# First layer's entry: x rows loaded first, the norm's squares between the columns, two convolutions in two token ranges

## The chip, the cores and the metric

The program runs on one core of a Trainium2 chip. A core has a matrix engine (TensorE, PE in the profile), and three engines that work on up to 128 partitions at once: VectorE (DVE), ScalarE (ACT) and GpSimd (POOL). SyncE (SP) issues most of the transfers between HBM and the on-chip memory SBUF; TensorE writes to a second memory, PSUM, which VectorE and ScalarE read. Each engine works through its own instructions in order and waits on semaphores for the others. The metric is the device time of one execution in microseconds (us), as the median of several runs.

## The reference

One step of a trunk with two layers: a Mamba-2 layer (SSD), then a layer of latent attention (MLA), each on a prompt of 1024 tokens and on a sample group of 8 x 8 tokens, 1088 tokens in all, of width 1024. The part that the change touches is the beginning of the first layer:

```python
def rms_norm(x, w):
    xf = x.astype(F32)
    y = xf * lax.rsqrt(jnp.mean(xf * xf, axis=-1, keepdims=True) + NORM_EPS)
    return (y * w.astype(F32)).astype(x.dtype)

def causal_conv(xbc, buf, w, b):
    t = xbc.shape[1]
    full = jnp.concatenate([buf.astype(xbc.dtype), xbc], axis=1)
    out = full[:, 0:t] * w[0]
    for k in range(1, SSD_CONV_W):
        out = out + full[:, k:k + t] * w[k]
    return out + b, full[:, full.shape[1] - (SSD_CONV_W - 1):]
...
def ssd_mixer(h, conv_buf, ssm_state, w_in, conv_w, conv_b, dt_bias, a_log, d_skip, norm_w, w_out):
    b, t, _ = h.shape
    proj = jnp.einsum('btd,de->bte', h, w_in)
    z = proj[..., :SSD_D_INNER]
    xbc = proj[..., SSD_D_INNER:SSD_D_INNER + SSD_CONV_DIM]
    dt_raw = proj[..., SSD_D_INNER + SSD_CONV_DIM:]
    xbc, new_buf = causal_conv(xbc, conv_buf, conv_w, conv_b)
    xbc = jax.nn.silu(xbc.astype(F32))
```

The rows x are normed by the root of their mean square, multiplied by the input weights, and 4096 of the resulting columns go through a causal convolution over four tokens and a SiLU. Everything is float32. The output of the whole is the normed result, the new SSM and convolution states and the new cache rows.

## The kernel before

A float32 product is made of three products of operands split in a high and a low part: high x high, low x high and high x low. So every operand is split: ScalarE writes the high part (for x: `xh`, for weights: `wih`), and VectorE or GpSimd the low part (`xl`, `wil`). The split of weights is at lines 129 and 130; the raw weights (`wraw`) come by a transfer at line 276.

The tokens are cut in three ranges, of 384, 384 and 320 tokens (range 0, 1 and 2), and in nine tiles of 128 rows (the last has 64), three tiles to a range. The norm of the first layer goes range by range (`norm_steps`). `norm_rows` loads a range's tiles `xt` (line 694 for the prompt, 696 for the sample group), lets ScalarE square each and sum it (line 223, result `ssq`), VectorE add the small constant (line 203), GpSimd raise it to the power -1/2 (line 208), and VectorE scale the rows (line 228). `norm_cols` then takes the eight groups of 128 columns, called columns 0 to 7 here: TensorE transposes the three tiles into PSUM (line 238, `xtp`, two buffers), ScalarE multiplies by the norm's weight and writes the high part (line 239, `xh`), VectorE the low part (line 240, `xl`). As columns of a range become ready, TensorE multiplies them with the first two blocks of weights (line 88, `pj`): six products to a column, three for each block. A block is 128 of the output columns. The blocks 0 and 1 of the first group run through all three ranges side by side with the norm; block 2 and the rest follow.

The rows of a range are normed while the range before is projected: in the program, `norm_rows` of range i + 1 is called behind `norm_cols` of range i. What a piece of product leaves in PSUM, ScalarE copies to a buffer `raw` (line 458 for ranges 0 and 1, 460 and 461 for range 2), of which there are two. When a block's three pieces are there, ScalarE begins the convolution (line 471: the last of four taps, with the bias), and VectorE adds the other three taps, one step each over 1112 columns (line 474). Only then is the buffer `raw` free for the next block but one: block 2 takes that of block 0. Between these stand, on VectorE, the low part of a weight block, and on GpSimd low parts of the weights of block 2 (line 130) and of the gates (line 335).

Other loads at the entry, in the order of the program: the identity `ident` (line 138), `alog` (line 160, with an exponential on ScalarE at line 161, which brings the loading of an activation table), the vectors of the convolution and the norms (lines 183 to 188), masks (167 to 173), `dtb` and `dsk` (175, 176), and the convolution's state `cst` (311), which TensorE transposes (line 316, `cvp`).

The order of an engine's instructions is set by a planner, which works from estimated costs of its own and from the program's order, unless a stretch of the program states for an engine that the written order stands (`manual_schedule`). Before the change that is used for two late places only. The same code of the norm serves the second layer (there with `tail`, line 864 being a gate beside it), and the planner orders that as well.

## Time and profile before

| | us |
|---|---|
| median of 3 runs | 2012.39 |
| lowest and highest run | 2009.29, 2013.6 |
| profiled execution | 2011.21 |
| its span in the profile | 2009.4 |
| TensorE busy | 1916.5 (95%) |
| VectorE busy | 1198.7 (60%) |
| ScalarE busy | 1109.7 (55%) |
| GpSimd busy | 826.6 (41%) |

The profile is one execution; its span is 1.8 us shorter than its device time. A row of a timeline gives start, length, engine, line, operation, output and inputs, and in brackets how long the engine was idle before it and what ended that. In rows of transfers, SPq is the queue of SyncE. "x3" puts three of a kind in a row together. A TensorE row's length reaches beyond the start of the next, since products overlap.

### The profile page before, as it was taken

The numbers are of one execution on the slowest core, as the hardware profiler recorded it, in microseconds if no ns is written. First come the engines' busy times: TensorE is split into PE (matmuls) and PEld (weight loads), VectorE is DVE, ScalarE is ACT, GpSimd is POOL, SyncE is SP. The second block draws the span as 40 slices with busy tenths as digits, with TensorE's granted clock in tenths as the row PEclk, the third lists the DMA queues.
The fourth block names the chain that finished last, engine by engine and source line by source line (L and its number), as shares of the span: only waits on it lengthen the run. The fifth ranks groups of instructions, "written<-read, shape, count | busy, mean of one in ns | idle before, by whom it ended". The sixth has DMA issues, their size and how long they took to land. (4 is left out here: it accounts for less than half of the span.)

```text
span 2009.4 us, 33417 instructions
## 1 busy us (share of the span) xinstructions
PE 1916.5 (95%) x12001; PEld 1739.9 (87%) x12001; DVE 1198.7 (60%) x2431; ACT 1109.7 (55%) x2535; POOL 826.6 (41%) x1007
## 2 busy tenths in 40 slices
PE   6999999999999999898998999999999999889998
PEld 5899999999999999786777999898888888778887
DVE  4537565656575656755333204465787877676675
ACT  5456767666666666733114314335777777655552
POOL 1327555555655555542002213103343435755551
PEclk9999999999999999899999999999999999899999
DMA  4213333333323332646544333132121113544541
GB/s 150 58 52 93 90 86 92 83 95 84 95 82 94 82 94 66 199 154 198 158 142 133 125 145 90 62 108 73 50 66 40 50 42 91 176 148 142 146 145 37
DMA packets 182460, 206.58 MB, mean 103 GB/s; under 512 B 18988, under 2 KB 147896, under 8 KB 181912
## 3 DMA queue, kind: packets, MB, share of 16 engines
q1 hardware_dynamic: 177240, 184.67, 30.9%
q0 software_dynamic: 4976, 19.66, 3.1%
q8 instruction: 95, 1.56, 0.3%
q14 instruction: 69, 0.57, 0.1%
q10 hardware_dynamic: 80, 0.13, 0.0%
HBM read 151.10 MB, written 53.28 MB: 102 GB/s over the span
## 5 line engine op out<-in xcount | busy, mean ns | idle before, releaser
L88 PE MATMUL pj<-xh,wih 128*128 128x384 f32 (+1 forms) x768 | 256.4, 338 | 9.5 <-ACT xh L239 4.9
L88 PE MATMUL pj<-xl,wih 128*128 128x384 f32 (+1 forms) x768 | 255.3, 333 | 0.0
L88 PE MATMUL pj<-xh,wil 128*128 128x384 f32 (+1 forms) x768 | 254.8, 332 | 0.0
L474 DVE SCALAR_TENSOR_TENSOR acc<-raw,vec,acc 128x1112 f32<-128x1112 f32 x96 | 141.2, 1475 | 25.7 <-ACT acc L471 24.9
L88 PEld LDWEIGHTS pj<-xh,wih 128*128 128x128 f32 x768 | 145.7, 191 | 11.7 <-ACT xh L239 5.5
L1283 POOL TENSOR_TENSOR tl<-P,th 128x384 fp32r<-128x384 f32 (+1 forms) x96 | 91.7, 956 | 155.4 <-ACT P L1281 113.6
L88 PEld LDWEIGHTS pj<-xl,wih 128*128 128x128 f32 x768 | 146.4, 191 | 0.9
L88 PEld LDWEIGHTS pj<-xh,wil 128*128 128x128 f32 x768 | 146.0, 190 | 0.4
L100 PE MATMUL pz<-wih,xh 128*128 128x256 f32 x504 | 142.5, 286 | 0.0
L100 PE MATMUL pz<-wil,xh 128*128 128x256 f32 (+1 forms) x504 | 140.1, 284 | 0.0
L1280 ACT ACTIVATE th<-st 128x512 fp32r<-128x512 f32 x192 | 94.5, 492 | 71.2 <-PE st L1276 52.0
L577 ACT ACTIVATE M<-M,tok 128x128 f32<-128x128 f32 (+1 forms) x288 | 90.6, 386 | 70.3 <-DVE M L574 69.8
L100 PE MATMUL pz<-wih,xl 128*128 128x256 f32 x448 | 128.3, 286 | 0.0
L1572 POOL TENSOR_TENSOR kvl<-pgr,kvh 128x1024 fp32r<-128x1024 f32 x32 | 77.6, 2426 | 70.5 <-ACT kvh L1571 70.5
L100 PEld LDWEIGHTS pz<-wih,xh 128*128 128x128 f32 x504 | 95.8, 190 | 0.3
L574 DVE TENSOR_TENSOR M<-M,negu 128x512 f32<-128x512 f32 x64 | 51.2, 800 | 70.7 <-DMA M<-acs_d 70.2
L1281 ACT ACTIVATE P<-st 128x512 f32<-128x512 f32 x192 | 93.4, 486 | 0.0
L100 PEld LDWEIGHTS pz<-wil,xh 128*128 128x128 f32 (+1 forms) x504 | 92.7, 184 | 0.8
L130 DVE TENSOR_TENSOR wil<-wraw,wih 128x512 fp32r<-128x512 f32 x88 | 71.6, 823 | 31.0 <-ACT wih L129 29.7
L1283 DVE TENSOR_TENSOR tl<-P,th 128x512 fp32r<-128x512 f32 x96 | 72.9, 759 | 21.5 <-ACT P L1281 20.8
L100 PEld LDWEIGHTS pz<-wih,xl 128*128 128x128 f32 x448 | 85.2, 190 | 0.1
L560 POOL TENSOR_TENSOR xdd<-xsT,tok 128x256 f32<-128x256 f32 x64 | 51.0, 797 | 73.3 <-ACT xsT L546 73.0
(820 smaller groups left out, 6326.8 us busy)
## 6 DMA issues: line engine op xcount, KB each, us to landing
wraw<-in_ssd_w_in SPq DMA_DIRECT2D x92, 256.0 KB
M<-acs_d SPq DMA_DIRECT2D x64, 256.0 KB
s<-in_state_ssm SPq DMA_DIRECT2D x32, 256.0 KB
y_d<-y SPq DMA_DIRECT2D x64, 128.0 KB
out_s_ssm<-s SPq DMA_DIRECT2D x32, 256.0 KB
wraw<-in_ssd_w_out SPq DMA_DIRECT2D x16, 512.0 KB
q_d<-qt SPq DMA_DIRECT2D x32, 192.0 KB
qp<-q_d SPq DMA_DIRECT2D x8, 768.0 KB
```

The lines of the kernel that those rows point to most:

```text
L88: nc.tensor.matmul(out, a, b, start=(i == 0), stop=(i == n - 1))
L100: nc.tensor.matmul(o, a, b, start=(j == 0), stop=(j == len(ops) - 1))
L130: (eng or nc.vector).tensor_tensor(lo, src, hi.bitcast(F32), op=ALU.subtract)
L474: nc.vector.scalar_tensor_tensor(acc, raw[:, j : j + n], k.convw[j][:, blk : blk + 1], acc, op0=ALU.mult, op1=ALU.add)
L560: nc.gpsimd.tensor_tensor(v3(xdd), v3(xsT), hb(2), op=ALU.mult)
L574: nc.vector.tensor_tensor(M[:m, :, :m], M[:m, :, :m], (k.negs if smp else k.negu)[:m, :m].unsqueeze(1).to_broadcast([m, 4, m]), op=ALU.add)
L577: nc.scalar.activation(M[:m, h, :m], M[:m, h, :m], AF.Exp, bias=tk[:, 0, 4 * g + h : 4 * g + h + 1])
L1280: nc.scalar.activation(th[:, :n], ps[:, :n], AF.Exp, scale=SCALE)
L1281: nc.scalar.activation(P[:, :n], ps[:, :n], AF.Exp, scale=SCALE)
L1283: eng.tensor_tensor(tl[:, :n], P[:, :n], th[:, :n].bitcast(F32), op=ALU.subtract)
L1572: nc.gpsimd.tensor_tensor(rl, raw, rh.bitcast(F32), op=ALU.subtract)
```

## The change

Three things are changed in the first layer's entry.

The transfers of the first three x tiles are issued ahead of those of `ident` and `alog`; `ident` now goes with the vectors, and `alog` and its exponential with the masks.

The square of a tile of the next range is no longer called behind all columns of the present range but between them: `norm_rows` becomes a generator (`rows_steps`), of which one step (a load and a square) follows each column from column 2 on (`LATE = 2`). In the first layer the whole norm stands under `manual_schedule` for ScalarE, so that ScalarE takes its instructions there in the order in which the program states them. In the second layer (`tail`) the steps are still taken behind the columns.

The convolutions of blocks 0 and 1 of the first group are done in two ranges of tokens: 768 columns as soon as ranges 0 and 1 are in `raw`, the other 344 at the end.

```diff
+LATE = 2
...
-    nc.sync.dma_start(k.ident, I["c_ident"])
...
-    nc.sync.dma_start(k.alog, k.I["ssd_a_log"][0].partition_broadcast(128))
-    nc.scalar.activation(k.alog, k.alog, AF.Exp)
...
     nc.gpsimd.memset(k.yssq, 1.0)
+    nc.sync.dma_start(k.alog, I["ssd_a_log"][0].partition_broadcast(128))
+    nc.scalar.activation(k.alog, k.alog, AF.Exp)
...
     nc, I, cp = k.nc, k.I, k.cp
+    nc.sync.dma_start(k.ident, I["c_ident"])
...
-def norm_rows(k, gi, load, pool, xbufs, pre=None):
+def norm_rows(*a):
+    xs = []
+    drain(rows_steps(xs, *a))
+    return xs
+
+
+def rows_steps(xs, k, gi, load, pool, xbufs, pre=None):
...
         xs.append((xt, m, TILES[i][0] - t0))
+        yield
...
     for gi in range(3):
-        norm_cols(k, gi, rows, wcol, hi, lo, psum)
-        if gi < 2:
-            rows = norm_rows(k, gi + 1, load, pool, xbufs, pre[gi + 1])
+        cols, nxt = norm_cols(k, gi, rows, wcol, hi, lo, psum), []
+        more = rows_steps(nxt, k, gi + 1, load, pool, xbufs, pre[gi + 1]) if gi < 2 else iter(())
+        for d, _ in enumerate(cols):
+            if not tail and d >= LATE:
+                next(more, None)
+        drain(more)
+        rows = nxt
...
+        def conv(a, b):
+            nc.scalar.activation(acc[:, a:b], raw[:, 3 + a : 3 + b], AF.Identity, bias=k.convb[:, blk : blk + 1],
+                                 scale=k.convw[3][:, blk : blk + 1])
+            for j in range(3):
+                nc.vector.scalar_tensor_tensor(acc[:, a:b], raw[:, j + a : j + b], k.convw[j][:, blk : blk + 1],
+                                               acc[:, a:b], op0=ALU.mult, op1=ALU.add)
+
         for ci in range(3):
             if ci == 2:
+                if g == 0 and bi < 2:
+                    conv(0, 768)
...
-        n = RAW - 3
-        nc.scalar.activation(acc, raw[:, 3:], AF.Identity, bias=k.convb[:, blk : blk + 1],
-                             scale=k.convw[3][:, blk : blk + 1])
-        for j in range(3):
-            nc.vector.scalar_tensor_tensor(acc, raw[:, j : j + n], k.convw[j][:, blk : blk + 1], acc,
-                                           op0=ALU.mult, op1=ALU.add)
+        conv(768 if g == 0 and bi < 2 else 0, RAW - 3)
...
-            norm_steps(k, x_loader(k), None, k.xh, k.xl, p0, psum, [st0], XB, before, after)
+            with tc.manual_schedule(engines={nc.scalar.engine}):
+                norm_steps(k, x_loader(k), None, k.xh, k.xl, p0, psum, [st0], XB, before, after)
```

Since the planner orders the rest, its effect is best seen in the order of an engine's instructions. First ScalarE in range 0 of the first layer, from the casts of the weights (`wih`) on. Before:

```order
L129 COPY wih<-wraw 128x512 x4
L223 ACTIVATE sq_218,ssq_214<-xt_216 128x1024
L239 ACTIVATE xh<-xtp_0_166,vec 128x384
L239 ACTIVATE xh<-xtp_1_172,vec 128x384
L223 ACTIVATE sq_222,ssq_214<-xt_220 128x1024
L223 ACTIVATE sq_226,ssq_214<-xt_224 128x1024
L239 ACTIVATE xh<-xtp_2_178,vec 128x384
L129 COPY wih<-wraw 128x512
L239 ACTIVATE xh<-xtp_3_184,vec 128x384
L239 ACTIVATE xh<-xtp_4_190,vec 128x384
L239 ACTIVATE xh<-xtp_5_196,vec 128x384
```

and after (line 229 is now the square, 245 the high part, 130 the cast):

```order
L130 COPY wih<-wraw 128x512 x4
L245 ACTIVATE xh<-xtp_0_166,vec 128x384
L245 ACTIVATE xh<-xtp_1_172,vec 128x384
L245 ACTIVATE xh<-xtp_2_178,vec 128x384
L229 ACTIVATE sq_188,ssq_184<-xt_186 128x1024
L130 COPY wih<-wraw 128x512
L245 ACTIVATE xh<-xtp_3_190,vec 128x384
L229 ACTIVATE sq_198,ssq_184<-xt_196 128x1024
L245 ACTIVATE xh<-xtp_4_200,vec 128x384
L229 ACTIVATE sq_208,ssq_184<-xt_206 128x1024
L245 ACTIVATE xh<-xtp_5_210,vec 128x384
```

The three squares of range 1's tiles moved from among columns 0 to 2 to among columns 2 to 5; the fifth cast still stands ahead of column 3. Second, VectorE at the same place, with the low parts (line 240, after 246) and the scaling of range 1's tiles (line 228, after 235). Before:

```order
L240 TENSOR_SCALAR xl<-xtp_2_178,vec,xh 128x384
L228 TENSOR_SCALAR xt_216<-xt_216,rs_228 128x1024
L228 TENSOR_SCALAR xt_220<-xt_220,rs_228 128x1024
L228 TENSOR_SCALAR xt_224<-xt_224,rs_228 128x1024
L240 TENSOR_SCALAR xl<-xtp_3_184,vec,xh 128x384
L240 TENSOR_SCALAR xl<-xtp_4_190,vec,xh 128x384
L240 TENSOR_SCALAR xl<-xtp_5_196,vec,xh 128x384
L240 TENSOR_SCALAR xl<-xtp_6_202,vec,xh 128x384
```

and after:

```order
L246 TENSOR_SCALAR xl<-xtp_4_200,vec,xh 128x384
L204 TENSOR_SCALAR rs_216<-ssq_184 128x3
L246 TENSOR_SCALAR xl<-xtp_5_210,vec,xh 128x384
L235 TENSOR_SCALAR xt_186<-xt_186,rs_216 128x1024
L235 TENSOR_SCALAR xt_196<-xt_196,rs_216 128x1024
L235 TENSOR_SCALAR xt_206<-xt_206,rs_216 128x1024
L246 TENSOR_SCALAR xl<-xtp_6_222,vec,xh 128x384
```

The scaling moved from behind column 2 to between columns 5 and 6. In range 1 it moves likewise, from behind column 3 to between 5 and 6. Other moves at the entry: on ScalarE the copies to `raw` of range 1 now stand ahead of the first `xh` of range 2 (before, behind it); on SyncE a third transfer of block 2's and 3's weights stands ahead of the four of `cst` (before, behind them). On VectorE the steps of the two convolutions alternate, and up to the step that frees block 0's buffer there are now three steps of 768 columns of each block, three of 344 of block 0, two of 344 of block 1 and one weight subtraction; before, three steps of 1112 columns of block 0, two of block 1 and the same subtraction.

Third, ScalarE in the norm ahead of the second layer, whose program text is the same, where the planner's order came out otherwise (`hh` is the high part there, `gt` the gates, `ck` weights). Before:

```order
L223 ACTIVATE sq,ssq_12448<-xt_12393 128x1024
L239 ACTIVATE hh<-xtp_7_12442,vec 128x384
L223 ACTIVATE sq,ssq_12448<-xt_12394 128x1024
L223 ACTIVATE sq,ssq_12448<-xt_12395 128x1024
L129 COPY ck2h<-wraw 128x288
L864 ACT_TABLE_LOAD
L864 ACTIVATE gt_12468<-pj 128x384
L129 COPY ck3h<-wraw 128x288
L864 ACTIVATE gt_12501<-pj 128x384
L223 ACTIVATE sq,ssq_12576<-xt_12397 128x1024
L239 ACTIVATE hh<-xtp_0_12528,vec 128x384
```

and after:

```order
L245 ACTIVATE hh<-xtp_7_12453,vec 128x384
L229 ACTIVATE sq,ssq_12459<-xt_12404 128x1024
L229 ACTIVATE sq,ssq_12459<-xt_12405 128x1024
L880 ACT_TABLE_LOAD
L880 ACTIVATE gt_12479<-pj 128x384
L880 ACTIVATE gt_12512<-pj 128x384
L229 ACTIVATE sq,ssq_12459<-xt_12406 128x1024
L229 ACTIVATE sq,ssq_12587<-xt_12408 128x1024
L229 ACTIVATE sq,ssq_12587<-xt_12409 128x1024
L229 ACTIVATE sq,ssq_12587<-xt_12410 64x1024
L130 COPY ck2h<-wraw 128x288
L245 ACTIVATE hh<-xtp_0_12539,vec 128x384
```

The third square moved behind the gates, and the squares of the range after next moved ahead of the first `hh`. The order of the last scan beside the first half of the output projection also came out otherwise.

3 lines of the change are left out of this document (1 added, 2 removed).

## The prediction

> **What bounds the kernel now.** I read the page first, then the chain of waits of TensorE, and then the timelines of TensorE, ScalarE, VectorE, GpSimd and the DMA queue over the first 75 us, since the change lies there. The page says that TensorE is the bound: 95% busy over the span.
>
> ```profile
> PE 1916.5 (95%) x12001; PEld 1739.9 (87%) x12001; DVE 1198.7 (60%) x2431; ACT 1109.7 (55%) x2535; POOL 826.6 (41%) x1007
> ```
>
> So only idle of PE, or a lower clock of PE, moves the end. The waits of PE, summed by what it waited for (total, times, longest), show how little there is:
>
> ```profile
> PE xtp L238 <- DVE xt L228: 5.7, 3, 3.2
> PE poa L100 <- ACT yha L129: 5.6, 3, 3.2
> PE pj L88 <- ACT xh L239: 4.9, 2, 3.0
> PE pj L88 <- ACT raw L458: 4.3, 2, 4.0
> ```
>
> The third and fourth row are the first layer's entry, 9.2 us together; the first has its longest wait in the same norm before the second layer, and the second lies in the first half of the output projection. The entry on PE's timeline (start, length, what it waited for in brackets):
>
> ```profile
> 12.41 2.02 PE L238 MATMUL xtp<-ident,xt 128*128 128x128 f32 x6 [2.26 <-DVE xt L228]
> 17.44 1.01 PE L88 MATMUL pj<-xh,wih 128*128 128x384 f32 x2 [3.02 <-ACT xh L239]
> 24.36 0.52 PE L88 MATMUL pj<-xh,wih 128*128 128x384 f32 x2
> 28.51 0.51 PE L88 MATMUL pj<-xh,wih 128*128 128x384 f32 x2
> ...
> 29.13 0.42 PE L88 MATMUL pj<-xl,wih 128*128 128x384 f32 x1
> 31.35 0.82 PE L238 MATMUL xtp<-ident,xt 128*128 128x128 f32 x6
> 34.02 0.61 PE L88 MATMUL pj<-xh,wih 128*128 128x384 f32 x2 [1.86 <-ACT xh L239]
> 47.01 0.42 PE L88 MATMUL pj<-xh,wih 128*128 128x320 f32 x1
> 57.68 0.45 PE L88 MATMUL pj<-xh,wih 128*128 128x384 f32 x1 [0.29 <-ACT raw L461]
> ...
> 70.54 0.41 PE L88 MATMUL pj<-xh,wih 128*128 128x320 f32 x1 [4.04 <-ACT raw L458]
> ```
>
> In order: first product of range 0 at 17.44, of its column 3 at 24.36 and column 6 at 28.51 (so 1.38 us a column), the low part of column 6 at 29.13, its end at 31.35; range 1 from 34.02, range 2 from 47.01, block 2 from 57.68 with its third piece at 70.54. Below I follow these marks, and the sum is how far each moves.
>
> **The first columns.** ScalarE and the DMA queue:
>
> ```profile
> 0.73 1.28 ACT L161 ACT_TABLE_LOAD   x1 [0.73 <-PEq L1912]
> 6.32 1.06 ACT L223 ACTIVATE sq<-xt 128x1024 f32<-128x1024 f32 x1 [1.28 <-DMA xt<-in_x_prompt]
> 15.77 1.06 ACT L223 ACTIVATE sq<-xt 128x1024 f32<-128x1024 f32 x1 [1.83 <-DMA xt<-in_x_prompt]
> 16.83 1.03 ACT L239 ACTIVATE xh<-xtp,vec 128x384 fp32r<-128x384 f32 x2
> 22.73 0.62 ACT L129 CAST wih<-wraw 128x512 fp32r<-128x512 f32 x1 [2.32 <-DMA wraw<-in_ssd_w_in]
> 23.25 1.19 ACT L239 ACTIVATE xh<-xtp,vec 128x384 fp32r<-128x384 f32 x2
> ```
> ```profile
> 0.74 0.39 SPq L138 DMA_DIRECT2D ident<-in_c_ident  x1
> ...
> 1.65 1.38 SPq L694 DMA_DIRECT2D xt<-in_x_prompt  x3
> 18.74 0.93 SPq L276 DMA_DIRECT2D wraw<-in_ssd_w_in  x2
> ```
>
> *x first.* ident and alog leave from ahead of the x rows, so these are issued at 0.74 instead of 1.65, 0.91 us sooner, and land at about 5.3. But the table load, which ran at 0.73 while nothing was there to do, now stands behind the first square's wait: 5.3 + 1.28 = 6.6 against 6.32. The lead is spent, and the first square comes 0.3 later; so do the transposes (12.7 to 14.7). The Trainium skill, "ScalarE: Activation LUTs", section "What ACT_TABLE_LOAD costs", gives 1.28 us for the load and 1.38 more for a drain, 2.66 in all; by it the first square would stand at 8.0, and the mark at 17.44 would gain 1.4 less. Row 0.73 has the load alone, and nothing in it shows a drain. What hides the small loads (alog, ident) is that their readers come later: ident by the transposes of the vectors, alog far behind.
>
> *Squares behind the first columns.* The first two xh pieces stood behind the square at 15.77, which waited 1.83 us for its x rows. Now three xh pieces stand ahead of it, and the first runs when its transposes end, 14.6, plus 0.55 (1.03 for two): product at 15.2, 2.2 us sooner than 17.44. But the next xh piece, of column 3, stands behind the cast of a weight part that landed at 22.7. Its transfer was issued at 18.74, behind the same x rows in the queue; nothing moves it by more than some 0.4. So xh 3 is ready at 23.25 + 0.6 = 23.85, and column 3 starts at 23.9 instead of 24.36: of 2.2 us 0.5 is left, the rest turns into idle before column 3.
>
> **The later columns of range 0.** Now ScalarE does xh 3, square, xh 4, square, xh 5. The square at 15.77 held ScalarE for 1.06 until 16.83, and two xh took 1.03, so a column costs it about 1.55 where PE needs 1.38. xh 5 is ready at 23.85 + 2 x 1.55 = 26.95. VectorE:
>
> ```profile
> 21.12 2.08 DVE L228 TENSOR_SCALAR xt<-xt,rs 128x1024 f32<-128x1024 f32 x3
> 27.24 0.62 DVE L240 SCALAR_TENSOR_TENSOR xl<-xtp,vec,xh 128x384 fp32r<-128x384 f32 x1 [0.77 <-ACT xh L239]
> 59.26 4.99 DVE L474 SCALAR_TENSOR_TENSOR acc<-raw,vec,acc 128x1112 f32<-128x1112 f32 x3 [3.26 <-ACT acc L471]
> 64.17 3.15 DVE L130 TENSOR_TENSOR wil<-wraw,wih 128x512 fp32r<-128x512 f32 x1
> ```
>
> The scaling of the next x rows (2.08 us) moves from behind xl 2, where PE had a clock of half and work in hand, to behind xl 5 and ahead of xl 6. It starts when xl 5 ends, 27.55, ends at 29.65, and xl 6 is ready at 30.25. PE needs it for the mark at 29.13, so this mark moves by +1.1, and range 0 ends at 32.45. If the weight part comes 0.4 sooner, +0.7; if the scaling waits longer for the power on GpSimd, +1.6. The transfer of the conv state now stands behind one more weight part in the queue; its transposes are wanted just ahead of the same mark, and it costs nothing unless it lands after 29.9.
>
> The power on GpSimd, between the sum of squares and the scaling, is this row; with the small step ahead of it some 1.2:
>
> ```profile
> 20.22 0.87 POOL L208 TENSOR_TENSOR rs<-rs,nhalf 128x3 f32<-128x3 f32 x1 [1.05 <-DVE rs L203]
> ```
>
> **Range 1.** Its first xh no longer stands behind the square that waited for x rows (that wait is the 1.86 idle before 34.02). From 32.45: two copies and an xh, about 0.5 each on ScalarE, first product at 34.1, +0.1. ScalarE then does the three squares between columns 2 to 5 at 1.55 a column, and the scaling stands again ahead of xl 6. By the same spacing as in range 0 the third square ends seven columns' work later, near 40; 1.2 for the power, scaling to 43.35, xl 6 at 44.0, where PE, 6 columns of 1.38 and the half of one behind 34.1, would want it at 42.9: +1.1. In the kernel before, this stage took from 34.02 to near 45.9, 0.8 more than eight columns at 1.38. End +0.4.
>
> **Range 2 and block 2.** The copies of range 1 now stand ahead of the first xh of range 2 (before, behind it): one copy's 0.5 and a bit, +0.6. Range 2 itself is PE's own work, so block 2 starts at 57.68 + 1.0 = 58.7.
>
> **The two convolutions in two token ranges.** What holds PE until 70.54 is a raw buffer that VectorE frees with block 0's last convolution step. Rows of ScalarE and GpSimd, and the page's mean of a step:
>
> ```profile
> 57.88 2.55 ACT L471 ACTIVATE acc<-raw,vec 128x1112 f32<-128x1112 f32 x2
> 70.00 0.86 ACT L458 COPY raw<-pj 128x384 f32<-128x384 f32 x2 [8.55 <-DVE acc L474]
> ```
> ```profile
> 63.03 3.74 POOL L335 TENSOR_TENSOR zdl<-wraw,zdh 128x1152 fp32r<-128x1152 f32 x1
> 69.95 0.11 POOL L454 MEMSET raw<- 128x3 f32 x1 [3.18 <-DVE acc L474]
> ```
> ```profile
> L474 DVE SCALAR_TENSOR_TENSOR acc<-raw,vec,acc 128x1112 f32<-128x1112 f32 x96 | 141.2, 1475 | 25.7 <-ACT acc L471 24.9
> ```
>
> VectorE worked from 59.26 to 69.95, 10.69 us, on five steps of 1112 columns and a subtraction (the sixth step comes behind). That stretch is VectorE's own and is not waiting for PE. In the changed order the first two steps of 768 columns run under PE's last columns and their copies; the Identity of block 1's first part, 0.9 of the 1.28 that one took at 57.88, ends 1.0 + 0.6 later than that row begins, at 59.45. From 59.45 there are left 4 x 768 + 5 x 344 = 4792 columns instead of 5560, at 1.475/1112 = 1.33 ns a column 1.02 us less, and four instructions more. What an instruction costs beyond its columns no row gives; between nothing and 0.2 each I take 0.1 (xl of 384 columns 0.62). So 59.45 + 10.69 - 1.02 + 0.4 = 69.5: the buffer comes free 0.4 sooner, and PE starts at 70.1, between 69.2 and 71.1. The split pays back the 1.0 that the norm lost, and little more: the mark at 70.54 moves by -0.4. PE's gap shrinks from 4.04 to about 2.6.
>
> **The clock behind the gap.** After the gap PE ran at half clock for 3.3 us, worth 1.65:
>
> ```profile
> 71.10:74.40 3.30, 3.30 (x14) 3.30 (x14) 0.08 (x1) 3.29 (x3) 0.92 (x4) 0.50 0.45 129
> ```
> ```profile
> 1376.60:1378.10 1.50, 0.09 (x1) 0.00 (x0) 0.34 (x3) 0.89 (x3) 1.05 (x2) 1.00 0.62 174
> 1379.20:1381.20 2.00, 2.00 (x9) 1.71 (x8) 0.69 (x1) 0.38 (x3) 1.94 (x3) 0.50 1.11 362
> ```
>
> (PEclk is the third number from the right.) The second pair shows the clock halve after a gap of only 1.5 us, so a gap of 2.6 doesn't save this stage for certain; I leave it in. The Trainium skill, "TensorE: Matmul & The Clock Gate", section "What's actually happening", has the clock halve only after one idle window of about 3.4 us, by windows that run freely. By that rule a gap of 2.6 keeps full clock and the sum is 1.65 less. The trace speaks against it with the row at 1379.20.
>
> **Behind the entry.** The planner orders the rest anew. Instructions and counts are the same, the order differs in the last scan beside the output projection (I count 0, with 5.6 us of waits there, the second row of the waits, as room) and in the norm ahead of the second layer:
>
> ```profile
> 1092.99 1.06 ACT L223 ACTIVATE sq<-xt 128x1024 f32<-128x1024 f32 x1 [4.22 <-DMA xt<-h_d]
> 1097.17 1.28 ACT L864 ACT_TABLE_LOAD   x1
> 1099.17 0.49 ACT L864 ACTIVATE gt<-pj 128x384 f32<-128x384 f32 x1
> 1101.74 0.58 ACT L239 ACTIVATE hh<-xtp,vec 128x384 fp32r<-128x384 f32 x1 [0.96 <-PE xtp L238]
> ```
>
> There the third square goes behind the table load and two gates, and three more squares ahead of the first hh. Square 1 starts at 1092.99 when its row lands, square 2 ends by 1095.7, load (1.28) and two gates (0.49 each) by 1097.9; four squares of 1.06 to 1102.2, a cast, so hh at about 1102.7 instead of 1101.74: +1.0. It is +2.1 if the scaling behind the third square, which now starts near 1097.9 instead of 1095.8, sets it; and near 0 if the waits behind it shrink in return.
>
> **The sum.** Entry -0.4 (from -1.3 to +0.6), last scan 0, second norm +1.0: 2011.21 + 0.6 = 2011.8 against the profiled run, which lies 1.2 below the median 2012.39 (its span is 2009.4, 1.8 outside it). Against the median: 2013.0.
>
> **Rivals.** (1) *The lead stays.* If the weight part lands early enough for column 3, the 2.2 us are kept through range 0, 1.0 of the 1.86 goes too, GpSimd and VectorE start as much sooner, and the shorter gap saves the half clock: -2.2 - 1.0 - 1.65 = -4.8, 2007.6. Against it: row 22.73 and the two-us scaling. Chance 0.20. (2) *The clock lags (slower).* New short gaps before columns 3 to 6 keep the clock at half there: from 17.44 to 24.36 three columns took 2.3 each, against 1.38, four columns +3.7, on top of +0.6: 2016.7. It decides from gaps of 1.5 us on in one window, as at 1376.6. Chance 0.15. (3) *The planner's order decides.* One more wait in the last scan like the longest there, 3.2, gives +3.8, and with the second norm at its +2.1 +4.9, 2017.3; chance 0.12. (4) *The forecast*, within 0.2% (4.0 us, about what a measurement of this kernel can tell from no change): 0.53. That the entry does nothing measurable is this case.
>
> So faster 0.20, same 0.53, slower 0.27. For 8 in 10 the range reaches beyond both sides of the rivals by the spread of the runs shown (2009.29 to 2013.6): 2007 to 2018.5; the forecast's own is 2010.5 to 2015.5.
>
> **What would show it.** First product near 15.2; idle of 1 to 2 us before column 3; xl 6 right behind three scalings; range 1 at 33.8 to 34.6; block 2 at 58.2 to 59.5; the third piece at 69.2 to 71.1 after a gap of 2 to 3.3. I'm wrong if column 3 starts before 22, if block 2 starts before 57.5, if half clock is seen between 24 and 31, or if the times behind 75 us shift by more than 3 us.

## The result, and the profile after

The changed kernel takes 2018.22 us (median of six runs, 2015.89 to 2021.27); the kernel before, run beside it, 2010.87 (six runs, 2009.29 to 2013.6). The ratio is 1.0033 with a 95% interval of 1.0020 to 1.0047, so it is slower by some 6.6 us. The forecast was 2013.0, no measurable change. The time lies outside the 2010.5 to 2015.5 that the forecast called its own, and only 0.3 us inside the wide range of 2007 to 2018.5; the whole interval lies above 1, and the way the time moved, slower, had a chance of 0.27.

The profiled execution of the changed kernel took 2021.27 us, the longest of the six, with a span of 2019.3; that of the kernel before 2011.21, with 2009.4. Of the 9.9 us between the two spans some 3 therefore belong to this one execution, and a difference that stands in a single pair of profiles proves little. The first line of the page:

```profile
PE 1917.4 (95%) x12001; PEld 1740.2 (86%) x12001; DVE 1200.1 (59%) x2437; ACT 1109.5 (55%) x2537; POOL 828.0 (41%) x1007
```

TensorE's work is the same, 1917.4 us against 1916.5. What grew by 9.0 is the span beside it, 101.9 us against 92.9. The waits of TensorE (total, times, longest, in us), after:

```profile
PE xtp L244 <- DVE xt L235: 9.0, 2, 6.2
...
PE act L1646 <- DVE ac L1639: 6.3, 1, 6.3
PE pj L89 <- ACT xh L245: 5.1, 4, 3.5
PE pj L89 <- ACT raw L469: 4.3, 2, 4.0
```

and one row of the same view of the kernel before, which the prediction did not quote:

```profile
PE act L1630 <- DVE ac L1623: 4.4, 1, 4.4
```

The wait for `raw` (the convolution) is unchanged at 4.3 with a longest of 4.0; the waits for `xh` at the entry are about as many us as before (5.1 against 4.9), with the longest, 3.5, now ahead of column 3; `xtp <- xt` has 9.0 instead of 5.7, 6.2 of it in the norm ahead of the second layer; and `act <- ac`, in the sample stage of the attention near 1770 us, has 6.3 instead of 4.4. The prediction had looked at all of these places but the last.

The entry on TensorE's timeline after, the marks of the prediction in the same order (start, length, in brackets the idle time and what ended it):

```profile
14.64 1.01 PE L89 MATMUL pj<-xh,wih 128*128 128x384 f32 x2 [0.58 <-ACT xh L245]
24.94 0.62 PE L89 MATMUL pj<-xh,wih 128*128 128x384 f32 x2 [3.47 <-ACT xh L245]
35.10 0.62 PE L89 MATMUL pj<-xh,wih 128*128 128x384 f32 x2 [0.43 <-ACT xh L245]
44.87 0.44 PE L89 MATMUL pj<-xl,wih 128*128 128x384 f32 x1 [0.62 <-DVE xl L246]
...
60.06 0.45 PE L89 MATMUL pj<-xh,wih 128*128 128x384 f32 x1 [0.29 <-ACT raw L472]
72.83 0.41 PE L89 MATMUL pj<-xh,wih 128*128 128x320 f32 x1 [3.95 <-ACT raw L469]
```

| mark | before | after | moved | forecast |
|---|---|---|---|---|
| first product of range 0 | 17.44 | 14.64 | -2.80 | -2.2 |
| column 3 | 24.36 | 24.94 | +0.58 | -0.5 |
| range 1 | 34.02 | 35.10 | +1.08 | +0.1 |
| range 2 | 47.01 | 48.53 | +1.52 | +0.6 at the end |
| block 2 | 57.68 | 60.06 | +2.38 | +1.0 |
| third piece of block 2 | 70.54 | 72.83 | +2.29 | -0.4 |

The first product starts 2.8 us sooner, and TensorE has lost all of it and more by column 3. ScalarE and SyncE's queue show where:

```profile
4.50 1.28 ACT L229 ACT_TABLE_LOAD   x1 [4.50 <-DMA xt<-in_x_prompt]
5.80 1.06 ACT L229 ACTIVATE sq<-xt 128x1024 f32<-128x1024 f32 x1
...
23.79 0.62 ACT L130 CAST wih<-wraw 128x512 fp32r<-128x512 f32 x1 [5.52 <-DMA wraw<-in_ssd_w_in]
24.32 0.57 ACT L245 ACTIVATE xh<-xtp,vec 128x384 fp32r<-128x384 f32 x1
```
```profile
19.04 7.13 SPq L287 DMA_DIRECT2D wraw<-in_ssd_w_in  x3
```

ScalarE stands idle for 5.52 us, until 23.79, for the weights of its fifth cast. These are weights of block 2, wanted at 60 us; but the cast stands ahead of the `xh` of column 3 in ScalarE's order, so column 3 waits for them. Their transfer is issued at 19.04 (18.74 before), and they land 1.06 us later than before (cast at 22.73 there); why so much later is left open, since the issue accounts for 0.3. After the idle 3.47 us TensorE's clock falls, which the windows of the changed kernel show (length, busy us of each engine, then the granted clock as the third number from the right):

```profile
25.00:27.00 2.00, 1.97 (x10) 1.64 (x11) 1.11 (x2) 2.00 (x4) 0.78 (x1) 0.84 0.03 7
27.00:30.00 3.00, 3.00 (x13) 2.87 (x12) 2.23 (x6) 1.49 (x4) 0.91 (x2) 0.54 0.74 211
```

That is 0.32 and 1.38 us of full speed lost, 1.7 in all, in a stretch where the kernel before ran at full clock.

### The profile page after: what moved, and what is told of

Read it like the earlier page. It is cut to its first block, busy times and chain, and to the rows that moved or that the text cites. A ratio compares the mean times of both kernels' runs of the same rounds, so it can differ in the third digit from the quotient of the medians.

```text
span 2019.3 us, 33425 instructions
## 1 busy us (share of the span) xinstructions
PE 1917.4 (95%) x12001; PEld 1740.2 (86%) x12001; DVE 1200.1 (59%) x2437; ACT 1109.5 (55%) x2537; POOL 828.0 (41%) x1007
## 5 line engine op out<-in xcount | busy, mean ns | idle before, releaser
L478 DVE SCALAR_TENSOR_TENSOR acc<-raw,vec,acc 128x1112 f32<-128x1112 f32 (+2 forms) x102 | 143.5, 1413 | 22.6 <-ACT acc L475 21.7
L89 PEld LDWEIGHTS pj<-xh,wih 128*128 128x128 f32 x768 | 146.1, 191 | 12.1 <-ACT xh L245 6.2
L101 PEld LDWEIGHTS pz<-wil,xh 128*128 128x128 f32 (+1 forms) x504 | 92.9, 185 | 0.8
```

Of the source, the lines that this page charges most:

```text
L89: nc.tensor.matmul(out, a, b, start=(i == 0), stop=(i == n - 1))
L101: nc.tensor.matmul(o, a, b, start=(j == 0), stop=(j == len(ops) - 1))
L478: nc.vector.scalar_tensor_tensor(acc[:, a:b], raw[:, j + a : j + b], k.convw[j][:, blk : blk + 1], acc[:, a:b], op0=ALU.mult, op1=ALU.add)
```

## Experiments

A shift below is the start of the same TensorE instruction in that run's profile less its start in the kernel before's (2009.4 us of span). Ratios are to the kernel before on the same chip.

Every profile is of one execution, and its rows scatter. In the eight profiles that load x first and have the cast ahead of column 3, column 3 lies between 24.10 and 25.77; in the seven of them with squares between the columns, block 2 lies between 59.24 and 61.57. Of the kernel before there is one profile (24.36 and 57.68). So a mark of one pair that differs by about 1 us doesn't show a cause by itself.

**The order behind the entry, with the entry nearly as it is.** The planner's order of everything behind the first layer depends on `LATE`: with 1 it is row for row the order of the kernel before behind the entry, with 3 that of the changed kernel.

```diff
-LATE = 2
+LATE = 1
```

> All three parts of the change, but the squares begin behind column 1 instead of column 2. The planner's order behind the entry then comes out as in the kernel before. Theory 'entry' (most of the 7 us comes from the entry, by what it sets off later): block 2 still starts 2 us later than before, and the time is 5 to 8 us above the kernel before. Theory 'order' (the entry costs 2.3 us, the new order in the last scan, the norm ahead of the second layer and the sample stage the rest): 1 to 3 us above. Theory 'chance' (half-clock stages fall otherwise from run to run): the drift behind 80 us stays within 2 us of either sign.

```diff
-LATE = 2
+LATE = 3
```

> The squares begin behind column 3; the planner's order behind the entry is that of the changed kernel, word for word. Theory 'order': 6 to 9 us above the kernel before, as the changed kernel. Theory 'entry': depends on where block 2 starts; the scaling now stands ahead of the low part of column 7 instead of 6, so block 2 starts 1.5 to 3 us later than before, and the time goes with it, 5 to 8 us above.

Measured: 1.0011 (0.9998 to 1.0024) for 1, and 1.0042 (1.0025 to 1.0058) for 3. The entry goes the other way: block 2 moved by +2.71 with 1 and by +1.81 with 3. So the kernel that reaches block 2 later is the faster one, by 0.3% (the two intervals just miss each other), and what stands behind the entry weighs more between these two than the 0.9 us at block 2. In us they are +2.2 and +8.4; the theory of the order expected 1 to 3 and 6 to 9, that of the entry 5 to 8 for both.

**x first alone.** The kernel before, with only the transfers moved:

```diff
-    nc.sync.dma_start(k.ident, I["c_ident"])
...
-    nc.sync.dma_start(k.alog, k.I["ssd_a_log"][0].partition_broadcast(128))
-    nc.scalar.activation(k.alog, k.alog, AF.Exp)
...
+    nc.sync.dma_start(k.alog, I["ssd_a_log"][0].partition_broadcast(128))
+    nc.scalar.activation(k.alog, k.alog, AF.Exp)
...
+    nc.sync.dma_start(k.ident, I["c_ident"])
```

> Only the x rows go first, with alog and the identity behind; nothing else of the change. The order behind the entry differs from before in a few rows of the last scan only. Expected by all: first square at 5.8 instead of 6.32 (the table load stands behind the x row), first product where it was, 16.5 to 17.5, since a square that waits for the fourth x row still stands ahead of it; block 2 within 0.5 us of 57.68. Theory 'order': time within 2 us of the kernel before.

Measured: 1.0015 (1.0002 to 1.0028). The first product comes at 17.24, since two squares still stand among the first columns; column 3 at 25.40, 1.04 later than before; block 2 at 58.49 (+0.81). The fifth cast starts at 24.25 instead of 22.73. That is 1.5 later, though within the scatter given above; that loading x first makes the weight part land later is likely, then, and not shown. By itself it gains nothing: +3.0 us (expected within 2), and block 2 later by more than the expected 0.5.

**Without the split of the convolutions.** The changed kernel with the whole convolution at the end, as before:

```diff
-        def conv(a, b):
...
-                if g == 0 and bi < 2:
-                    conv(0, 768)
...
-        conv(768 if g == 0 and bi < 2 else 0, RAW - 3)
+        n = RAW - 3
+        nc.scalar.activation(acc, raw[:, 3:], AF.Identity, bias=k.convb[:, blk : blk + 1],
+                             scale=k.convw[3][:, blk : blk + 1])
+        for j in range(3):
+            nc.vector.scalar_tensor_tensor(acc, raw[:, j : j + n], k.convw[j][:, blk : blk + 1], acc,
+                                           op0=ALU.mult, op1=ALU.add)
```

> x rows first and squares between the columns, but the two convolutions whole. The mark of block 2's third piece tells the worth of the split: if the split gives back 1 us, it stands at 73.5 to 74.5 here against 72.83 in the changed kernel; if the split gives nothing, at 72.8. Block 2 starts at 60.0 as in the changed kernel. The order behind is a third one, neither that of before nor that of the changed kernel; theory 'entry': 6 to 9 us above before; theory 'order': anything from 1 to 8.

Measured: 1.0035 (1.0021 to 1.0049). From block 2 to its third piece it takes 12.87 us (59.24 to 72.11), and 12.86 in the kernel before; with the split 12.77. The split is worth 0.1 us. (The mark itself is 0.7 sooner than with the split, because this execution reached block 2 0.8 sooner.) This kernel also came out with a third order behind the entry, in which the second norm costs 4.7 us, so its total says nothing on the split.

**The same split four columns apart.** The planner's order flips on small numbers: a split at 764 keeps the changed kernel's order behind the entry, one at 760 gives a third order. Its sample stage is that of the kernel before, its last scan nearly so, and its second norm is that of the changed kernel but for two rows.

```diff
-                    conv(0, 768)
+                    conv(0, 764)
...
-        conv(768 if g == 0 and bi < 2 else 0, RAW - 3)
+        conv(764 if g == 0 and bi < 2 else 0, RAW - 3)
```

> The changed kernel with the first token range of the convolutions cut at 764 columns instead of 768. The order of the instructions behind the entry stays that of the changed kernel. All theories: as the changed kernel, 6 to 9 us above the kernel before.

> The same with the cut at 760. Four columns more or less cost nothing on the chip (5 ns a step), but in the planner's estimate they tip the order behind the entry: last scan, output projection and sample stage are ordered as in the kernel before, and only the norm ahead of the second layer stays as in the changed kernel. Theory 'order': 2 to 4 us above the kernel before, and 3 to 5 us below the cut at 764. Theory 'entry' or 'chance': like the cut at 764 within 1.5 us.

Measured: 1.0030 (1.0013 to 1.0047) with 764 and 1.0024 (1.0010 to 1.0037) with 760. They are 1.2 us apart, where the theory of the order expected 3 to 5 and its rival at most 1.5; the error covers both. The traces show why the pair doesn't test the sample stage alone. There 760 has the short stretch of the kernel before and 764 the long one, as shown below. But in the second norm 760 has a weight cast on ScalarE ahead of a `hh`, and a low part on VectorE, at other places than 764; from 1080 to 1200 us its shift grows by 3.4 us, that of 764 by 0.7. What 760 saves at the one place it loses at the other.

**What the split ran into.** The changed kernel without GpSimd's subtraction for the first group's gates (`zdl`); a memset, early, takes its place, so the low part of these weights is left out of the gates and step sizes.

```diff
-        nc.gpsimd.tensor_tensor(lo, raw, hi.bitcast(F32), op=ALU.subtract)
+        nc.gpsimd.memset(lo.bitcast(F32), 0.0)
```

> The changed kernel without GpSimd's subtraction that makes the low part of the gates' first weights (it is set to zero, early, in idle time): leaves out the low x high part of those gates. Theory 'taking turns' (VectorE's two-input steps and GpSimd's subtractions hold each other up, so the early steps only push GpSimd back): the weight subtraction on VectorE falls from 3.14 to below 1.5 us, and block 2's third piece starts 2 to 3 us sooner against block 2's start, 10 to 11 us behind it instead of 12.8. Rival (VectorE's own work or a wait for weights sets the end): 12.3 to 12.9.

The changed kernel first, VectorE and GpSimd from the convolution steps to the freeing of the buffer (the memset of `raw`):

```profile
58.75 7.99 DVE L478 SCALAR_TENSOR_TENSOR acc<-raw,vec,acc 128x768 f32<-128x768 f32 x7 [0.36 <-ACT acc L475]
66.66 3.14 DVE L131 TENSOR_TENSOR wil<-wraw,wih 128x512 fp32r<-128x512 f32 x1
69.72 2.95 DVE L478 SCALAR_TENSOR_TENSOR acc<-raw,vec,acc 128x344 f32<-128x344 f32 x5
```
```profile
60.08 1.02 POOL L489 COPY ct<-raw 128x24 f32<-128x24 f32 x1
...
61.98 1.94 POOL L345 CAST zdh<-wraw 128x1152 fp32r<-128x1152 f32 x1
...
66.32 2.93 POOL L346 TENSOR_TENSOR zdl<-wraw,zdh 128x1152 fp32r<-128x1152 f32 x1
72.25 0.11 POOL L465 MEMSET raw<- 128x3 f32 x1 [3.00 <-DVE acc L478]
```

Without the subtraction, VectorE, TensorE, and TensorE's clock behind the gap:

```profile
58.52 7.08 DVE L478 SCALAR_TENSOR_TENSOR acc<-raw,vec,acc 128x768 f32<-128x768 f32 x7 [0.36 <-ACT acc L475]
65.53 0.69 DVE L131 TENSOR_TENSOR wil<-wraw,wih 128x512 fp32r<-128x512 f32 x1
66.14 3.99 DVE L478 SCALAR_TENSOR_TENSOR acc<-raw,vec,acc 128x344 f32<-128x344 f32 x5
```
```profile
70.29 0.41 PE L89 MATMUL pj<-xh,wih 128*128 128x320 f32 x1 [1.64 <-ACT raw L469]
```
```profile
72.00:75.00 3.00, 3.00 (x22) 3.00 (x21) 0.62 (x1) 3.00 (x5) 0.74 (x1) 1.00 0.00 0
```

With block 2 at 59.83 there, the third piece comes 10.46 us later, 2.3 less than with the subtraction. VectorE's subtraction of 512 columns takes 0.69 us without `zdl` and 3.14 beside it, where it ends 0.55 us behind GpSimd's (69.80 and 69.25). And GpSimd is slower beside VectorE's early steps: the same copy of 24 columns took 0.20 at 57.69 in the kernel before and takes 1.02 here, the same cast 1.15 there (58.23) and 1.94 here, so that `zdl` starts 3.3 us later (63.03 there). Measured from block 2, `zdl` ends at 9.19 after and at 9.09 before. So this pair of subtractions, not the columns of the convolution, holds the buffer's release in the changed kernel. In the kernel before the same pair ends 0.55 us apart as well (67.32 and 66.77), but no run took `zdl` out of that one, and none left out both the split and `zdl`; what the split would be worth without `zdl` is not shown. The time of this one execution was 2008.93 us, beside a median before of 2008.77; one execution settles nothing on the total.

**The entry with the cast out of the way.** The first half of block 2's weights is loaded and cast behind column 7 of range 0; the second half in `block`, when block 2 begins:

```diff
+    def weights(self, bi, part=None):
...
+        eng = k.nc.gpsimd if g == 0 and bi > 1 else None
+        if part is not None:
+            src = k.I["ssd_w_in"][0][512 * part : 512 * part + 512, col : col + 128]
+            return load_parts(k, self.wp, src, 4, 1, "wi", WB, self.raws.get(bi), RB, eng)
...
+        if len(ws) == 4:
+            ws = ws + self.weights(bi, 1)
...
             def after():
                 ssd_consts(k)
+                g0.pre[2] = g0.weights(2, 0)
```

First with two more edits: `LATE = 1`, which gives the order of the kernel before behind the entry, and one activation on a single column at the start, which brings the table load back to 0.73 us:

```diff
+    k.warm = cp.tile([128, 1], F32, name="warm")
+    nc.scalar.activation(k.warm, k.nhalf[:, 0:1], AF.Square)
...
-LATE = 2
+LATE = 1
```

> The three parts of the change with three repairs: the cast of block 2's first weight part goes behind the last column of range 0 instead of ahead of column 3; squares begin behind column 1; an activation of one column loads the table at the start. The order behind the entry is that of the kernel before. Theory of the entry's cost (the cast that waits for its weights, and the scaling ahead of a low part): first square at 4.5 instead of 5.8, column 3 starts at 21 to 22.5 instead of 24.9, block 2 at 56.5 to 58 instead of 60.06, so -1 to +0.5 against the kernel before, and the time with it, -2 to +1 us. If the entry's loss has another cause (the clock, the transfers), block 2 stays at 59.5 to 60.5.

Then the same with `LATE = 2`, which has the changed kernel's order behind the entry:

> The repaired entry of the kernel with the late cast, but with squares behind column 2 as in the change; behind the entry, the order is that of the changed kernel, word for word. Entry: block 2 at 56 to 57.5. Theory 'order' (the new order costs some 0.5 us in the norm ahead of the second layer and 3 to 4.5 in the sample stage): +1.5 to +3.5 us against the kernel before, 3 to 5 us above the kernel with the late cast. Theory 'entry alone' (the order behind costs nothing, the time follows block 2's start): -2 to 0 us, like the kernel with the late cast.

And last the cast's move alone, without the early table load, so that TensorE's and VectorE's orders are row for row those of the changed kernel, and ScalarE's but for this cast:

> The changed kernel with one edit: block 2's first weight part is loaded and cast behind column 7 of range 0 instead of ahead of column 3; TensorE's and VectorE's order is row for row that of the changed kernel, and ScalarE's differs by that one cast. Theory (the cast held column 3): no idle of TensorE before column 3 beyond 0.5 us where the changed kernel had 3.47; block 2 starts near 57.8 (60.06 in the changed kernel; 56.5 where the table was loaded early as well, which by 1.28 us of load leaves 57.8), and the time is about 2.3 us below the changed kernel's, 1.0022 of the kernel before. Rival (the early table load made the gain of the two repaired kernels): the first product stays near 14.6, but column 3 still waits some 3 us, block 2 starts near 60, and the time is 1.0033 again.

Measured: 0.9991 (0.9977 to 1.0005) for the first, 1.0033 (1.0020 to 1.0046) for the second, and 1.0010 (0.9997 to 1.0022) for the last. The first came as expected (-2 to +1 us). The second, +6.6 us, is above both of its theories (+1.5 to +3.5, and -2 to 0); the last is below its 1.0022, which is the edge of its interval. The entry of the last one on TensorE, and ScalarE's squares and the cast:

```profile
20.00 0.51 PE L89 MATMUL pj<-xh,wih 128*128 128x384 f32 x2
...
26.68 0.52 PE L327 MATMUL cvp<-ident,cst 96*128 96x96 f32 x4 [2.02 <-DMA cst<-in_state_conv]
...
31.87 0.62 PE L89 MATMUL pj<-xh,wih 128*128 128x384 f32 x2 [0.29 <-ACT xh L245]
...
56.85 0.44 PE L89 MATMUL pj<-xh,wih 128*128 128x384 f32 x1 [0.29 <-ACT raw L477]
```
```profile
18.11 0.58 ACT L245 ACTIVATE xh<-xtp,vec 128x384 fp32r<-128x384 f32 x1 [0.57 <-PE xtp L244]
...
24.24 0.61 ACT L130 CAST wih<-wraw 128x512 fp32r<-128x512 f32 x1
```

The `xh` of column 3, which stood at 24.32 behind the cast, now runs at 18.11, and column 3 starts at 20.00 instead of 24.94, with no idle of TensorE ahead of it. The next to be late is the convolution's state: its transposes (`cvp`) stand in TensorE's order ahead of the last columns, and wait 2.02 us for its transfer. That wait comes although the edit also brings this transfer forward in SyncE's queue: it is issued at 19.26 instead of 26.22, and the last of the three weight transfers goes behind it, at 26.22. (One row of GpSimd moves too.) With the half clock that follows (0.63 and 0.80 in the two windows from 27 to 33 us, 1.7 us lost), range 1 starts at 31.87 instead of 35.10: of 4.9 us 3.2 are left, and block 2 starts 3.21 sooner than in the changed kernel, by this one move. With the table load early as well it is 56.10 and 56.52, 0.3 to 0.8 more. These starts of block 2, 56.10 to 56.85, lie well clear of the scatter from 59.24 to 61.57. So the cast's place is the cause of the entry's loss, by more than was expected of it (57.8), and the table load a small part at most. The 3.2 are not a gain of 3.2 over the changed kernel by 90 us, though: the last kernel stands at +0.24 there, where the changed kernel stands at +2.33, since the half clock behind the convolution gap cost it 1.1 more than it cost the profiles of the kernel before and of the changed one.

**GpSimd's subtraction moved behind.** Since `zdl` held the split, two kernels state GpSimd's order by hand, so that it comes behind the work of blocks 2 and 3 (the first with `LATE = 1`, the second with 0; both with the repaired entry):

```diff
+        order = ExitStack()
+        order.enter_context(tc.manual_schedule(engines={nc.gpsimd.engine}))
         for _ in range(6):
             next(st0)
...
             load_zdt(k, p0)
+            order.close()
```

> The kernel with the late cast, and GpSimd's order stated so that its subtractions for the gates stand behind the third piece of block 2: nothing is left out. Third piece 10 to 11 us behind block 2's start instead of 12.8, so its mark at 66 to 67.5 instead of 68.88. What it could lose: the gates' weights come later, needed at 82. Order behind: norm ahead of the second layer and last scan as in the changed kernel, sample stage as in the kernel before. Theory 'order': -4 to -2 us against the kernel before; 'entry alone': -4.5 to -3.

> The same with the squares behind column 0. The entry hardly differs (block 2 within 1 us), the order in the sample stage is now that of the changed kernel. Theory 'order': 3 to 4.5 us above the run with GpSimd's subtractions late, 0 to +2 against the kernel before, and TensorE's marks shift by +1.5 to +3 between 1700 and 1800 us where the other shifts by -1 to -2. Theory 'entry alone': within 1.5 us of it.

Measured: 1.0057 (1.0044 to 1.0070) and 1.0060 (1.0039 to 1.0081), the slowest of all: +11.5 and +12.1 us, where the theory of the order expected -4 to -2 and 0 to +2. They lie 0.6 us apart, as the rival had it (within 1.5; the theory of the order 3 to 4.5), although their traces differ by the 2.2 us of the sample stage (below). The gap itself is gone: the third piece comes 8.83 us behind block 2, and TensorE stands 6.1 us ahead of the kernel before at 86 us. But the first group's gates now wait for their weights. TensorE in the first of the two:

```profile
87.27 0.54 PE L101 MATMUL pz<-zdh,xh 128*128 128x288 f32 x2 [1.96 <-POOL zdh L347]
...
91.20 0.61 PE L101 MATMUL pz<-zdl,xh 128*128 128x288 f32 x1 [2.27 <-POOL zdl L348]
```

By 120 us it stands at +2.6: 8.7 us given back. The subtraction can't go later without being waited for; whether it would fit earlier was not run. Less their shifts at 120 us the two are still 8.9 and 8.7 us slower than the kernel before, more than any rest in the table below. No row shown here explains it; they are left out of the table. The first one's profile ends at +5.6, about half of its 11.5; that execution, 2017.05 us, was the fastest of its five.

## Behind the entry

Eight kernels have, behind the entry, the order of the kernel before or that of the changed kernel. Their ratios as us of 2010, less the shift of TensorE at 120 us, leave what the rest costs:

| kernel | order behind | ratio as us | shift at 120 us | rest |
|---|---|---|---|---|
| `LATE` 1 | before's | +2.2 | +3.4 | -1.2 |
| x first (a few rows differ) | before's | +3.0 | +2.0 | +1.0 |
| cast late, `LATE` 1 | before's | -1.8 | -0.5 | -1.3 |
| the change | after's | +6.6 | +2.3 | +4.3 |
| `LATE` 3 | after's | +8.4 | +1.6 | +6.8 |
| split at 764 | after's | +6.0 | +4.5 | +1.5 |
| cast late, `LATE` 2 | after's | +6.6 | 0.0 | +6.6 |
| cast alone | after's | +2.0 | +0.2 | +1.8 |

The first three have a mean of -0.5, the other five of +4.2. Each ratio is uncertain by some 2.5 to 3.4 us, which is the spread within the groups; only the means can be used, and the 4.7 us between them is itself uncertain by some 2.5 (an estimate from the intervals). The cleanest pair is the late cast with `LATE` 1 and 2: shifts at 120 us of -0.5 and 0.0, and ratios of 0.9991 and 1.0033, whose intervals lie apart. Against it stands the cast alone, which has the order of the latter behind the entry and 1.0010. Of the kernels with a third order, the split at 760 has a rest of +1.7 and the kernel without a split one of +5.4. So that the order behind costs something is well supported, and how much is not well known. Two places in the traces account for about as much.

**The second norm**, ScalarE and TensorE after:

```profile
1101.59 1.28 ACT L880 ACT_TABLE_LOAD   x1
1102.89 0.87 ACT L880 ACTIVATE gt<-pj 128x384 f32<-128x384 f32 x2
1103.64 1.06 ACT L229 ACTIVATE sq<-xt 128x1024 f32<-128x1024 f32 x1
...
1108.64 1.52 ACT L245 ACTIVATE hh<-xtp,vec 128x384 fp32r<-128x384 f32 x3
```
```profile
1106.88 2.15 PE L244 MATMUL xtp<-ident,xt 128*128 128x128 f32 x9 [6.24 <-DVE xt L235]
1109.28 1.01 PE L89 MATMUL pj<-hh,wgh 128*128 128x384 f32 x2 [0.24 <-ACT hh L245]
```

and TensorE before, at the same two instructions:

```profile
1099.45 1.51 PE L238 MATMUL xtp<-ident,xt 128*128 128x128 f32 x6 [3.16 <-DVE xt L228]
...
1102.38 1.01 PE L88 MATMUL pj<-hh,wgh 128*128 128x384 f32 x2 [0.24 <-ACT hh L239]
```

The third square stands behind the table load and the gates, so the scaling that needs its sum is late, and TensorE waits 6.24 us instead of 3.16. The first product is then set by its `hh`, which starts at 1108.64 without a wait, behind the next range's three squares and a cast; before, at 1101.74, it had waited 0.96 us for transposes. TensorE comes to its long wait sooner, though: its shift is +5.91 at 1080, +4.35 where the wait begins (1096.29 and 1100.64), and +6.90 at the first product behind it, 1.0 more than at 1080. From 1080 to 1200 us the shift grows by 0.5 to 1.4 in the eight profiles that have this order (the first with GpSimd's subtraction moved among them), 0.8 in the mean, and by 0.0 in three of the kernel before's.

**The sample stage.** Here TensorE takes a product of scores (`sc`) and, some 12 us on, transposes a finished result (`act`), for which VectorE scales `ac`. Before, TensorE and VectorE:

```profile
1750.86 0.50 PE L88 MATMUL sc<-tk,qpr 96*128 96x512 f32 x1 [1.83 <-POOL tk L1489]
...
1763.07 0.66 PE L1630 MATMUL act<-ident,ac 128*128 128x128 f32 x2 [4.40 <-DVE ac L1623]
```
```profile
1757.93 0.47 DVE L1620 SCALAR_TENSOR_TENSOR ac<-ac,f,o 128x256 f32<-128x256 f32 x1
1758.44 4.49 DVE L1623 TENSOR_SCALAR ac<-ac,ln 128x256 f32<-128x256 f32 x1
1762.85 1.21 DVE L130 TENSOR_TENSOR ol<-og,oh 128x1024 fp32r<-128x1024 f32 x1
```

and in the kernel with the cast's move alone, which has the changed kernel's order here:

```profile
1751.87 0.50 PE L89 MATMUL sc<-tk,qpr 96*128 96x512 f32 x1 [1.84 <-POOL tk L1511]
...
1766.26 0.66 PE L1652 MATMUL act<-ident,ac 128*128 128x128 f32 x2 [6.33 <-DVE ac L1645]
```
```profile
1759.93 2.63 DVE L131 TENSOR_TENSOR ol<-og,oh 128x1024 fp32r<-128x1024 f32 x1 [0.66 <-ACT oh L130]
1762.49 0.47 DVE L1642 SCALAR_TENSOR_TENSOR ac<-ac,f,o 128x256 f32<-128x256 f32 x1
1762.88 2.97 DVE L1770 TENSOR_TENSOR w5l<-w5r,w5h 128x1024 fp32r<-128x1024 f32 x1
1765.77 0.34 DVE L1645 TENSOR_SCALAR ac<-ac,ln 128x256 f32<-128x256 f32 x1
```

Two subtractions that TensorE isn't waiting for, `ol` and `w5l`, now stand ahead of the last step of `ac` instead of behind it. From `sc` to `act` it is 12.2 us in the seven profiles with the kernel before's order here (12.18 to 12.24; the kernel split at 760 and the one without a split are among them) and 14.4 (14.39 to 14.42) in six of the seven with the changed kernel's; the seventh is the changed kernel itself, with 13.88 there and a longer stretch ahead of it (13.5 from the `sc` before, 11.0 to 11.2 in the others). So the order costs 2.2 us at this one place. Over the whole stage, 1690 to 1800 us, the shift falls by 0.9 to 1.5 in the three profiles with the kernel before's order throughout, and grows by 0.9 to 3.8 in the seven others, 2.5 in the mean; counted against the mean of the four that include the kernel before itself (-0.9), some 3.5 us, and 3.3 against all seven with that order here. Part of what is beyond the 2.2 may be the clock: in this stage the traces' record has half clock for 18.1 us in the mean of the profiles with the changed kernel's order and for 14.7 in the others, and half of these 3.4 us is lost. The two groups overlap (13.7 to 20.5, and 10.2 to 20.5), so this is an estimate from means and not shown.

Together 0.8 and 3.5, 4.3 us, against the 4.7 between the group means; the agreement is closer than either is known. The last scan (820 to 1000 us) moved by -0.8 in the mean of the eight profiles with the changed kernel's order there and by -1.5 in the three with the other, which is less apart than single profiles are (from -2.8 to +2.2). From 90 to 820 us the changed kernel's profile loses 3.8 us more, but others with the same order there gain up to 4.4 us; I put that down to the one execution.

So the change's 6.6 us are some 2.3 at the entry, where the cast's place is shown to be the cause, and some 4.3 behind it, in places whose program text did not change. Of these the 2.2 us between `sc` and `act` are shown row by row; the rest is argued from means.

## The prediction, point by point

*First square and first product: right in direction, better than forecast.* The forecast had the table load behind the first x tile, with the square 0.3 later than before; the rows are 4.50 and 5.80 instead of 6.6, since the tile landed at 4.5, not 5.3. The first product came at 14.64 instead of 15.2. The Trainium skill, "ScalarE: Activation LUTs", section "What ACT_TABLE_LOAD costs", would have 2.66 us from load to square; the trace has 1.30.

*Column 3: the mechanism right, the size wrong.* The text named the cast as what holds column 3, and wrote of its transfer that "nothing moves it by more than some 0.4". It was issued 0.3 later, and landed 1.06 later; x first alone had 1.5; why so much later stays open. So column 3 moved by +0.58 and not by -0.5, and the idle ahead of it was 3.47, not 1 to 2. This is the term of the sum that was mis-sized at the entry.

*Half clock at columns 4 to 6: rival 2's mechanism, beside the forecast.* The forecast left the clock full there and named half clock between 24 and 31 as what would make it wrong. It was seen from 26.4 to 29.8, 1.7 us of full speed lost, behind one gap of 3.47 and not behind the several short gaps that the rival spoke of. At its own 3.7 it was overpriced. Two of the signs that the text set for being wrong came true, then: this one, and that the times behind 75 us shift by more than 3 (4.1 at 240 us, 9.8 at 1800 in the profile).

*The convolution's state.* The forecast let it cost nothing unless it landed after 29.9. In the changed kernel TensorE came so late that it cost nothing; with the cast moved it was the next wait, 2.02 at 26.68.

*The scaling ahead of `xl` 6: right in place.* The three scalings ran from 28.61 to 30.69 in range 0, where TensorE at half clock was late enough not to wait, and at 42.21 in range 1, where it waited 0.62 (forecast 1.1).

*Ranges 1 and 2: too cheap.* From range 1 to block 2 the forecast adds 0.9 (0.4 by the end of range 1 less 0.1 at its start, and 0.6 for the copies); measured 1.30, and 1.0 to 1.4 in every kernel with this order of the squares and copies, 0 with x first alone (58.49 - 34.85, 23.64 against 23.66). The copies ahead of the first `xh` of range 2 also push the transposes of its column 2 behind the first products, which the text called "PE's own work".

*The split: the step that failed.* "The split pays back the 1.0 that the norm lost" rested on VectorE's stretch growing with its columns. It does not: 0.1 us came back, not 1.4. The prediction quoted both VectorE's subtraction (3.15) and GpSimd's beside it (3.74), and took them as fixed lengths. They end together, and GpSimd's work ahead of them is longer beside the early steps of VectorE. Without `zdl` the changed kernel takes 10.46 us instead of 12.77.

*The gap and the clock.* The forecast left the stage of half clock in at a gap of 2.6. The gap stayed at 3.95, so this wasn't put to the test by the change. Without `zdl` the gap was 1.64 and the clock stayed full (1.00 in 72 to 75 us), where the trace of before had halved it behind a gap of 1.5 at 1376.6. So the length of one gap doesn't decide it. By the Trainium skill, "TensorE: Matmul & The Clock Gate", section "What's actually happening", 1.64 us can't halve the clock; that run agrees, and the row at 1379.20 that the prediction quoted still doesn't.

*The second norm: right, in size and mechanism.* +1.0 forecast by its row-by-row working, with the squares ahead of the first `hh` as the reason; 0.8 in the mean of eight profiles, and the `hh` stands as it said.

*The rest of the planner's order: not examined.* Rival 3 put the price of a flipped order at one more wait of 3.2 in the last scan, and gave 2017.3 with a chance of 0.12. The mechanism and nearly the size are what happened (0.8 and 3.5); the place was another. The text named the last scan and the second norm as the places where the order differs, and put everything else at nothing without a reason: the order of VectorE in the sample stage had changed as visibly as ScalarE's in the norm, and the waits of TensorE before the change had `act <- ac` with 4.4 us in them.

*In sum*, by the forecast's own terms: entry -0.4, measured +2.3; second norm +1.0, measured +0.8; all else 0, measured +3.5. It comes to 6.6 in place of 0.6. That 2018.22 still falls into the range is luck: the range reached up to 2018.5 for rivals whose prices lay in other places, with the spread of the runs added, and the terms of the forecast don't lead there.

No version beat both kernels. The repaired entry with the order of the kernel before (0.9991, 0.9977 to 1.0005) beats the changed kernel; against the kernel before it is not told apart.

## What to carry to other kernels

An instruction that nobody needs soon (here a weight cast for 35 us later, `ol` and `w5l` ahead of the step that TensorE awaits) can cost as much as it waits for, as soon as it stands in an in-order engine ahead of one that is needed; ask of every row ahead of a critical one when its own input lands. Where a planner orders the whole program, a change in one place is also a draw of a new order for all the others, so compare the orders at every wait of the bounding engine, and compare measurements at equal order. Two rows that run side by side on two engines may hold each other up; don't scale one of them alone.

## What the runs showed of the hardware that was not expected

VectorE and GpSimd held each other up: VectorE's subtraction of 512 columns took 0.69 us without `zdl` and 3.14 beside it, and GpSimd's copy of 24 columns 0.20 us in the kernel before and 1.02 beside VectorE's convolution steps. In the sample stage even VectorE's small step `ac` (128x256, 0.34 us in one order) took 4.49 in the other and ended at 1762.9, as GpSimd's two subtractions there did (to 1762.8). The Trainium skill, "GPSIMD Engine Reference", section "Key points", says that GpSimd shares its interfaces to SBUF with VectorE, with contention for VectorE instructions in a 2-port performance mode or with two inputs from SBUF. The subtraction and the convolution steps, with two inputs each, agree; `ac` has one tile as its input, and no run shows which of the two holds there. At the split it was worth 2.3 us of TensorE's time.

TensorE's first products ran at half speed in a stretch where the view prints full clock. In the kernel before, a window of the entry:

```profile
20.00:23.00 3.00, 3.00 (x12) 2.90 (x11) 2.63 (x5) 0.68 (x2) 0.91 (x2) 1.00 0.87 220
```

Twelve instructions in 3 us, where the same kernel has 22 between 27 and 30 (transposes counted in both), at 1.00 in both. The trace's record of the clock begins only at 23.28 us here (at 19.54 in the changed kernel, at 17.53 with the cast alone), and a window ahead of it prints 1.00 for want of a record. In all three, products of 384 columns that follow each other start 0.32 us apart ahead of that time and 0.17 to 0.18 behind it. So the stretch ran at half speed, as the prediction read it. The Trainium skill, "TensorE: Matmul & The Clock Gate", section "What's actually happening", has the throttled state as the default, which activity releases; these rows agree.

The same instructions at the same places moved by several us between executions: from 240 to 1080 us kernels with one and the same order there drifted against the kernel before by +1.8 (the change) and by -5.2 (`LATE` 3).
